# Idle matmuls of 512 columns cut into quarters at the head of TensorE's stream, to move its instruction fetches by 102 instructions

## The chip, the cores and the metric

One core of one Trainium2 chip. The metric is the device time of one execution in microseconds (us), as the median of several; the profile's span, from the first to the last instruction, is some 2 us shorter.

## The reference

```python
batch, m, k, h, n = 16, 512, 768, 3072, 768        # x, w1, b1, w2: float32
y = np.matmul(x, w1) + b1
y = 0.5 * y * (1.0 + erf(y / np.sqrt(2.0)))        # exact GELU
return np.matmul(y, w2).astype(np.float32)
```

## The kernel before

Both products run in f16 by a scheme with seven instead of eight block products (the second in two levels), so VectorE forms sums of operands all the time and ScalarE and VectorE combine partial results. All instructions stand in an order fixed by hand. While the first tiles of x are on their way, TensorE runs idle matmuls on zeros (`spin`), from 1.19 us on. Its clock rises meanwhile: up to 4.63 us the idle matmuls of 512 columns start 427 ns apart, and later ones 216 (the record of the granted clock begins at 4.63 us, at 1.0); the dense matmuls begin at 10.06 us.

```python
for t in range(4):                                   # x tiles 0 to 3, by the hardware DMA queue
    nc.sync.dma_start(out=xf[:, t, :], in_=xr[:, t, :])
...
load_wt(1)                                           # w1 tile 1, by the software queue (POOL)
for t in range(4, 8):
    load_x(0, t)                                     # x tiles 4 to 7, the same queue
for n in range(2, 4):
    load_wt(n)

def spin(n):
    for k in range(n):
        nc.tensor.matmul(out=(bX[1], bY[1])[k % 2][:], lhsT=zero[:, 0, 0:P], rhs=zero[:, 0, :],
                         start=True, stop=True, skip_group_check=True)

spin(9)
for t in range(4):
    ...                                              # cast of x tile t on VectorE
    transpose_pe(0, t, ...)                          # six transposes on TensorE, then a copy
    ...
    spin(2)
...
class Unit1:                                         # dense matmuls of the first product
    def mm(self, p, dst, first, c0, c1):
        ...
        for c in range(c0, c1):
            nc.tensor.matmul(out=dst[:, 0:RH], lhsT=w1_op(self.wt, slot)[:, c, :],
                             rhs=a[:, c, :], start=first and c == 0, ...)
...
    def store(self, r):                              # output stores of the second product
        ...
        eng = nc.sync if self.sb + 1 == nsb and self.p != 2 else nc.gpsimd
        eng.dma_start(out=orr[...], in_=self.dst[:, r]...)
```

Of the kernel before, what the change touches and what calls it, by code (L numbers as in the profile page):

```python
# [10 lines left out]
P = 128  # L11
# [11 lines left out]
def kernel(  # L23
# [8 lines left out]
    nc = tc.nc  # L32
# [5 lines left out]
    RH = SB // 2  # L38
# [160 lines left out]
    bX = [pp.tile([P, 512], FP32, name=f"bX{k}") for k in range(2)]  # L199
    bY = [pp.tile([P, 512], FP32, name=f"bY{k}") for k in range(2)]  # L200
# [4 lines left out]
    with tc.manual_schedule():  # L205
# [539 lines left out]
        for half in range(2):  # L745
            r = slice(half * KQ, (half + 1) * KQ)
            nc.sync.dma_start(out=wf[:, r, :], in_=w1r[:, r, 0:2 * P])
        nc.scalar.dma_start(out=bf, in_=b1.rearrange("(hc p) -> hc p", p=P))
        zero = XTs[1][:, 0]
# [11 lines left out]
        def spin(n):  # L761

            for k in range(n):
                nc.tensor.matmul(out=(bX[1], bY[1])[k % 2][:], lhsT=zero[:, 0, 0:P], rhs=zero[:, 0, :],
                                 start=True, stop=True, skip_group_check=True)

        spin(9)
        for t in range(4):
            xhs[t] = xh_of(0, t)
            nc.vector.tensor_copy(out=xhs[t], in_=xf[:, t, :])  # L770
            transpose_pe(0, t, copy_halves if t == 3 else nc.scalar.copy)
            if t == 0:
                nc.tensor.transpose(out=bW[:, 0:2 * NH], in_=bf, identity=idf[0:2 * NH, 0:2 * NH])
                nc.scalar.copy(out=b1t[:], in_=bW[:, 0:2 * NH])
            spin(2)
# [402 lines left out]
```

## Time and profile before

| | before |
|---|---|
| median | 852.18 us (852.14 to 852.53, 3 runs) |
| span of the profiled run | 850.5 us |
| TensorE busy | 99% of the span |
| dense matmuls begin | 10.06 us |
| last matmul starts | 845.02 us |
| from there to the end of the span ("tail") | 5.50 us |
| instruction fetches of TensorE | 51 packets of 16384 bytes; the first at 19.24, the second at 38.73, the last at 844.30 us |

TensorE sets the time between the head and the tail, and the last matmul's start plus the tail is the span (845.02 + 5.50): what delays the last matmul and what comes after it can be read apart. The prediction below shows most of the lines behind this table. One thing that it shows only in numbers is how SyncE issued the last four output stores (start us, us that the issue took, queue, line, what):

```profile
842.54 0.37 SPq L550 DMA_DIRECT2D out_dram<-arena  x1
843.91 0.37 SPq L556 DMA_DIRECT2D out_dram<-arena  x1
844.90 1.04 SPq L550 DMA_DIRECT2D out_dram<-arena  x1
846.04 0.42 SPq L529 DMA_DIRECT2D out_dram<-arena  x1
```

Three issues take about 0.4 us and one 1.04. It starts while the last instruction fetch runs (844.30 to 845.54).

### The profile page before, as it was taken

The numbers are of one execution on the slowest core, as the hardware profiler recorded it, in microseconds if no ns is written. First come the engines' busy times: TensorE is split into PE (matmuls) and PEld (weight loads), VectorE is DVE, ScalarE is ACT, GpSimd is POOL, SyncE is SP. The second block draws the span as 40 slices with busy tenths as digits, with TensorE's granted clock in tenths as the row PEclk, the third lists the DMA queues.
The fourth block names the chain that finished last, engine by engine and source line by source line (L and its number), as shares of the span: only waits on it lengthen the run. The fifth ranks groups of instructions, "written<-read, shape, count | busy, mean of one in ns | idle before, by whom it ended". The sixth has DMA issues, their size and how long they took to land.

```text
span 850.5 us, 16682 instructions
## 1 busy us (share of the span) xinstructions
PE 842.8 (99%) x6504; PEld 573.4 (67%) x6504; DVE 673.3 (79%) x1134; ACT 426.3 (50%) x700; POOL 94.8 (11%) x151
## 2 busy tenths in 40 slices
PE   8999999999999999999999999999999999999997
PEld 5444445796544897449964599545995469944797
DVE  5766679777857997679967799668996699957997
ACT  4777763231287413773247721577126861277511
POOL 5021100042200002000020000210002100010000
PEclk9999999999999999999999999999999999999999
DMA  9998796699998699977999599995999949984497
GB/s 224 203 282 173 163 222 230 235 203 219 368 340 185 216 338 364 290 163 266 335 366 292 125 298 342 360 288 108 316 350 347 259 143 323 359 308 146 122 316 255
DMA packets 144819, 222.11 MB, mean 261 GB/s; under 512 B 61964, under 2 KB 85444, under 8 KB 144740
## 3 DMA queue, kind: packets, MB, share of 16 engines
q1 hardware_dynamic: 117392, 178.85, 66.6%
q0 software_dynamic: 27168, 42.08, 22.3%
q8 instruction: 51, 0.84, 0.4%
q14 instruction: 28, 0.23, 0.1%
q10 hardware_dynamic: 180, 0.11, 0.0%
HBM read 181.78 MB, written 49.45 MB: 272 GB/s over the span
## 4 chain that ended last, share of the span: by engine, by line
PE 98%; DMA 1%; ACT 0%; DVE 0%; SPq 0%; issue 0%
PE bY L414 21%; PE bY L518 15%; PE bX L414 14%; PE bX L518 10%; PE bW L414 7%; PE bZ L414 7%; PE bZ L518 5%; PE bW L518 5%; PE bY L457 4%; PE bZ L457 2%; PE bW L457 2%; PE bY L606 2%; PE bX L606 1%; PE bX L457 1%; DMA arena<-in_x_dram 1%; PE bZ L606 1%
## 5 line engine op out<-in xcount | busy, mean ns | idle before, releaser
L210 DVE TENSOR_TENSOR arena<-arena 128x1536 f16<-128x1536 f16 (+6 forms) x638 | 410.1, 674 | 5.7 <-ACT arena L335 0.9
L414 PEld LDWEIGHTS <-arena 128*128 128x128 f16 x1974 | 192.5, 98 | 224.0 <-issue 0.2
L518 PEld LDWEIGHTS <-arena 128*128 128x128 f16 x3528 | 292.1, 98 | 8.2
L414 PE MATMUL bY<-arena 128*128 128x512 f16 x846 | 214.4, 379 | 0.0
L637 DVE TENSOR_TENSOR arena<-bY,arena 128x512 f32<-128x512 f32 (+1 forms) x102 | 69.4, 681 | 118.1 <-PE bY L414 88.0
L630 ACT COPY bY<-bX 128x512 f32<-128x512 f32 (+1 forms) x145 | 79.6, 549 | 118.1 <-DVE arena L567 87.9
L518 PE MATMUL bY<-arena 128*128 128x192 f16 x1500 | 138.3, 246 | 0.0
L414 PE MATMUL bX<-arena 128*128 128x512 f16 x564 | 138.2, 379 | 0.0
L430 ACT ACTIVATE arena<-arena,b1t 128x1024 f16<-128x1024 f32 x94 | 108.0, 1149 | 51.6 <-DVE arena L665 51.6
L650 ACT COPY arena<-bW 128x512 f32<-128x512 f32 (+1 forms) x149 | 81.9, 550 | 92.9 <-PE bW L518 43.9
L518 PE MATMUL bX<-arena 128*128 128x192 f16 x1020 | 93.1, 246 | 0.0
L665 DVE TENSOR_TENSOR arena<-bZ,arena 128x512 f32<-128x512 f32 (+1 forms) x102 | 69.3, 679 | 21.4 <-PE bZ L414 18.2
L550 POOL DMA_DIRECT2D out_dram<-arena x42 | 30.5, 728 | 409.7 <-DVE arena L661 374.1
L414 PE MATMUL bW<-arena 128*128 128x512 f16 x282 | 76.2, 379 | 0.0
L414 PE MATMUL bZ<-arena 128*128 128x512 f16 x282 | 76.2, 379 | 0.0
L681 ACT COPY bZ<-bY 128x512 f32<-128x512 f32 (+1 forms) x60 | 31.8, 529 | 80.8 <-PE bY L457 30.0
L435 ACT ACTIVATE arena<-bX,b1t 128x512 f16<-128x512 f32 x94 | 64.0, 680 | 9.8 <-PE bX L414 9.7
L435 ACT ACTIVATE arena<-bY,b1t 128x512 f16<-128x512 f32 x94 | 63.3, 674 | 0.0
L457 PEld LDWEIGHTS <-arena 128*128 128x128 f16 x432 | 42.2, 98 | 28.0 <-issue 0.2
L319 POOL DMA_DIRECT2D arena<-in_x_dram x60 | 33.5, 626 | 156.3 <-DMA arena<-arena 146.9
L518 PE MATMUL bZ<-arena 128*128 128x192 f16 x504 | 48.5, 246 | 0.0
L518 PE MATMUL bW<-arena 128*128 128x192 f16 x504 | 48.5, 246 | 0.0
(63 smaller groups left out, 426.4 us busy)
## 6 DMA issues: line engine op xcount, KB each, us to landing
arena<-w2s SPq DMA_DIRECT2D x299, 288.0 KB, 4.6
arena<-w1s SPq DMA_DIRECT2D x72, 672.0 KB, 6.8
out_dram<-arena POOLq DMA_DIRECT2D x46, 384.0 KB, 7.1
w2s<-arena SPq DMA_DIRECT2D x49, 288.0 KB, 4.4
arena<-in_x_dram POOLq DMA_DIRECT2D x60, 192.0 KB, 7.7
w1s<-arena SPq DMA_DIRECT2D x12, 672.0 KB, 6.6
arena<-in_w_dram POOLq DMA_DIRECT2D x17, 384.0 KB, 8.4
out_dram<-arena SPq DMA_DIRECT2D x13, 384.0 KB, 2.5
```

What stands on the lines that cost most here:

```text
L210: nc.vector.tensor_tensor(out=o, in0=a, in1=b, op=op)
L319: nc.gpsimd.dma_start(out=xhs[t], in_=xr[:, sb * 8 + t, :])
L414: nc.tensor.matmul(out=dst[:, 0:RH], lhsT=w1_op(self.wt, slot)[:, c, :], rhs=a[:, c, :], start=first and c == 0, stop=c == self.C - 1, ski ...
L430: nc.scalar.activation(out=self.G[1][:, hi, :, :], in_=self.tmp, func=GELU, bias=b1t[:, 2 * hi + 1:2 * hi + 2])
L435: nc.scalar.activation(out=self.G[0][:, hi, row, :], in_=bank[:, 0:RH], func=GELU, bias=b1t[:, 2 * hi:2 * hi + 1])
L457: nc.tensor.matmul(out=dst[:, 0:N2], lhsT=a, rhs=w[:, :, c, :], start=first and c == 0, stop=c == self.C - 1, skip_group_check=True)
L518: nc.tensor.matmul(out=dst[:, t * N4:(t + 1) * N4], lhsT=a, rhs=w[:, c, :], start=first and c == 0 and t == ts[0], stop=c == NQ - 1, skip_ ...
L606: nc.tensor.matmul(out=dst[:, t * N4:(t + 1) * N4], lhsT=a, rhs=self.w[q][:, c, :], start=first and c == 0 and t == 0, stop=c == NQ - 1, s ...
L630: nc.scalar.copy(out=bY[u.g % 2][:, 0:u.F], in_=bX[u.g % 2][:, 0:u.F])
L637: nc.vector.tensor_tensor(out=u.c22(), in0=bY[u.g % 2][:, 0:u.F], in1=w[:, 0:u.F], op=ADD)
L650: nc.scalar.copy(out=w[:, 0:u.F], in_=bW[:, 0:u.F])
L665: nc.vector.tensor_tensor(out=u.c12(), in0=bZ[:, 0:u.F], in1=w[:, 0:u.F], op=ADD)
```

## The change

The idle matmuls stream the same columns, but each in four instructions with a weight load of their own. The work before the first real matmul should take the same time, and every later instruction stands 102 places further down, so that the fetches, which come some 255 instructions apart in the trace of before (on average; 51 of them for some 13,020 TensorE instructions), should fall 102 instructions sooner in the work.

```diff
         def spin(n):
             for k in range(n):
-                nc.tensor.matmul(out=(bX[1], bY[1])[k % 2][:], lhsT=zero[:, 0, 0:P], rhs=zero[:, 0, :],
-                                 start=True, stop=True, skip_group_check=True)
+                for r in range(0, RH, P):
+                    nc.tensor.matmul(out=(bX[1], bY[1])[k % 2][:, r:r + P], lhsT=zero[:, 0, 0:P],
+                                     rhs=zero[:, 0, r:r + P], start=True, stop=True,
+                                     skip_group_check=True)
```

## The prediction

Its sum came to 851.7 us (852.18 - 0.6 + 0.1). The pace that the prediction uses can be read off the trace of before between 11 and 845 us: matmuls of 128, 192, 256, 384 and 512 columns start on average 55.8, 82.6, 109.2, 162.5 and 215.9 ns after one of the same shape, which is 2.4 columns per ns plus 2.5 ns to within 0.2 ns. Up to 4.63 us, 512 columns took 427 ns; before has no row of 128 columns so early.

> **What bounds the kernel now.** I read the page's busy shares first, then TensorE's waits, then the chain of waits at the two ends of the span, and last the transfers there.
>
> ```profile
> span 850.5 us, 16682 instructions
> PE 842.8 (99%) x6504; PEld 573.4 (67%) x6504; DVE 673.3 (79%) x1134; ACT 426.3 (50%) x700; POOL 94.8 (11%) x151
> q8 instruction: 51, 0.84, 0.4%
> PE bX L764 <- DVE arena L750: 1.2, 1, 1.2
> PE bT L333 <- DVE arena L770: 0.7, 1, 0.7
> PE bT L333 <- ACT arena L335: 0.4, 1, 0.4
> ```
>
> TensorE is busy for 99% of the span and its three listed waits all lie in the first 10 us (the third column of a wait is the longest one). I also took the start-to-start distances of all 6504 matmuls from the trace and set each against the pace at which its shape runs in a stream (columns at 2.4 per ns plus 2.5 ns, which 512 columns keep at 216 ns). After 10.06 us only nine distances exceed it by over 30 ns, 0.65 us together, and six of those are one recurring place, "bX to bY" of the second product. So between 10 and 845 us TensorE loses nothing to its instruction fetches: the 51 fetches (0.84 MB, so 16 KB each) do not stall it. What a change to the fetches can win must then lie outside this stretch. That leaves the head and the tail.
>
> The head, in the chain of waits (start us, us, what):
>
> ```profile
> 1.67 5.22 DMA arena<-in_x_dram
> 6.89 0.02 issue
> 6.92 0.65 DVE arena L770
> 7.57 0.05 issue
> 7.62 0.52 PE bT L333 x6
> 8.14 0.02 issue
> 8.16 0.81 ACT arena L335
> 8.97 0.01 issue
> 8.98 0.52 PE bT L333 x6
> 9.50 0.02 issue
> 9.53 0.49 ACT arena L329
> 10.01 0.04 issue
> 10.06 0.81 PE bX L786 x3
> ```
>
> The idle matmuls (L764) are not in it. The arrival of x, its cast on VectorE, the transposes and ScalarE's copy set 10.06 us, where the dense matmuls begin. The idle matmuls fill TensorE's time beside that.
>
> The tail, by stretches (the last two columns are the mean busy share of the 16 DMA engines, and GB/s), and the transfer queues from 844.2 to 845.6 us:
>
> ```profile
> 844.30:845.55 1.25, 0.97 (x12) 0.74 (x9) 1.11 (x4) 0.00 (x0) 0.00 (x0) 1.00 0.94 327
> 845.85:846.29 0.44, 0.00 (x0) 0.00 (x0) 0.00 (x0) 0.00 (x0) 0.00 (x0) 1.00 0.05 14
> 846.30:848.25 1.95, 0.00 (x0) 0.00 (x0) 0.00 (x0) 0.00 (x0) 0.00 (x0) 0.86 0.89 308
> 848.30:849.00 0.70, 0.00 (x0) 0.00 (x0) 0.00 (x0) 0.00 (x0) 0.00 (x0) 0.50 0.06 21
> q8 instruction: 1, 0.02, 5.5%
> ```
>
> The last matmul starts at 845.0 us; from there on the output stores set the end. The last instruction fetch lies in the middle of them: one packet of 16384 bytes from 844.30 to 845.54 us. While it runs, the engine that carries it does no stores: of the store that ends then, 15 of 16 completion writes come by 845.25 us and one is missing. From 845.85 to 846.29 us fifteen engines have nothing to do and one catches up (a share of 0.05 is 0.8 of 16 engines). In the last stretch a share of 0.06 is again one engine of 16: its packets follow one another to 848.97 us, while those of the others end at 848.26 to 848.28. The sum fits: 1.24 us lost, some 0.44 caught up in the lull, 0.7 left over. The last landings read 848.65 us (the last of the even ones), then 849.03, 849.24 and 849.44 from the late engine. The program's end waits for the 849.44.
>
> [...]51 packets of 16384 bytes for some 13,020 TensorE instructions, on average 256 apart (single distances are 190 to 324). [...]That a long fetch holds up the store packets of its one engine is my reading of the tail above[...].[...]
>
> **The change part by part.** 17 idle matmuls (9, then 2 after each of four transposed tiles) become 68 of a quarter of the size. Columns and banks stay as they were. Added: 51 matmuls and 51 weight loads, 102 TensorE instructions at the head; the other engines' order is the same line for line.
>
> *The opening nine.* Before: starts 427 ns apart from 1.19 us; the clock doubles at 4.63 us (the granted clock in the trace). After: 107 ns apart (427/4), 32 of the 36 by 4.63 us, the last 4 in 0.22 us, so the transposes of tile 0 start at about 4.85 us against 4.83. Zero. If a cold weight load (151 ns by its record) did not hide, 23 would be done by 4.63 and the other 13 at 98 ns would take until 5.9 us. Tile 0 would then be one microsecond late; tile 2 waits for its x until 7.56 us and would start at most 0.3 us late, and tile 3 (8.98) has 0.59 us of idle TensorE ahead of it. So it would mostly be absorbed.
>
> *The four pairs.* 8 quarters at 55.6 are 0.44 us against 0.43. Ahead of 7.62, 8.98 and 10.06 us TensorE is idle for 0.88, 0.59 and 0.30 us, so the last pair may take 0.73 us, or 91 ns for each quarter. [...]Zero.
>
> *The fetches.* Each falls 102 instructions earlier in the work. I count that against the index of the instruction that runs as a fetch comes. For the last one: 13001 in the old numbering becomes 12899, which runs at 840.2 us. One standard deviation of the distances from the 256 grid is 21 instructions, here 0.9 us, so 839.3 to 841.1 us. Stores resume at 840.56 us after two idle microseconds of the queue. A fetch of about 0.95 us (its length on a quiet queue) from 840.2 makes its engine 0.6 us late at 841.15; the gap at 841.75 to 841.88 gives back 0.13 and the lull at 845.85 to 846.29 another 0.44. So next to nothing is left at the end: minus 0.79 us (849.44 to 848.65). If the fetch starts at 841 or later, 0.95 to 1.2 us are lost, minus 0.57 returned, leaving 0.4 to 0.6, so a gain of only 0.2 to 0.4. I take 0.6 us as the mean.
>
> The first fetch moves from 19.24 us to between 11 and 13.8 us (old index 133 runs at 13.6), into the loads of x tiles 4 to 7, which fill the queue (127% of the engines between 10 and 14 us, two of them at a time). These complete at 12.63, 13.58, 14.54 and 15.49 us, and their transposes start at 13.29, 14.27, 15.26 and 17.06, some 0.7 us later. A late engine (0.95 us) would stall TensorE by 0.25 us once. I count half of that, plus 0.1.
>
> Between, 49 fetches move by 4 to 11 us. None stalls TensorE today wherever it falls, so I count 0.
>
> Sum: 852.18 - 0.6 + 0.1 = 851.7 us.
>
> **The rivals.** (1) *Nothing happens*: the fetches are 0.4% of the transfers and TensorE never waits for one, so the time stays 852.2 within 0.2. For it: the 99%. Against it: the one late engine at the end. (2) *The quarters cost more than they hide*: cold or warm pairs issue-bound[...]. [...]Against it: pairs of 192 columns run at 82.5 ns, so two instructions cost no more than 41 each to issue, and the head's chain does not hold the idle matmuls.[...] (3) *A moved fetch strikes a load that a matmul is about to need*, in the head (+0.25) or in the middle (a few tenths): 852.0 to 852.4. (4) *The full gain without the cost*: 851.4.
>
> **Range and chances.** The reachable gain is 0.8 us, under 0.1% of the time, and the three runs of before spread by 0.39 us. The gain of 0.2 to 0.8, the head's cost of 0 to 0.25 and 0.2 of run-to-run noise give 851.1 to 852.2; for a stall in the middle or a costlier head I open the top to 852.4 and the bottom to 851.0. A change of 2% is 17 us, which nothing here can make: 1% either way.
>
> **What would show it.** In the profile after: the last matmul starts at 845.0 within 0.3; the clock rises near 4.63; dense matmuls begin at 10.06; the last fetch starts between 839 and 841.5; the last stretch with one busy engine is gone or shorter than 0.3 us, and the last landings lie together near 848.7; the span is about 850.0. The prediction is wrong if the tail keeps its late engine (then it was not the fetch), if a fetch still falls after 844 us, or if the dense matmuls begin later than 10.3.

## The result, and the profile after

The changed kernel took 852.16 us (851.62 to 852.5, 6 runs) against 852.16 (851.82 to 852.53, 6 runs) of the kernel before in the same rounds: ratio 0.9999, 95% interval 0.9987 to 1.0012. (A ratio is the mean time of one kernel's fast runs over that of the other's of the same rounds, so not quite the ratio of the medians.) So the time stayed, inside the range of the prediction and 0.46 us above its point.

The profile did not stay. The first line of its page, TensorE's waits, and the last fetch (queues between 839.5 and 840.6 us), where L414 is line 414 of the kernel:

```profile
span 850.0 us, 16784 instructions
PE bX L765 <- DVE arena L750: 1.2, 1, 1.2
PE bT L333 <- DMA arena<-in_x_dram: 0.8, 1, 0.8
PE bY L414 <- DVE bZ L683: 0.3, 1, 0.3
q8 instruction: 1, 0.02, 5.0%
```

There are still 51 fetches, now at 12.58, 30.19 and so on, the last at 839.63. Two waits are new: transposes wait for x itself, and dense matmuls (L414) for VectorE.

The tail in stretches that stand to the last matmul (845.92, it was 845.02) about as those of before, and SyncE's last four issues (start us, us that the issue took, queue, line, what):

```profile
845.20:846.45 1.25, 0.97 (x12) 0.74 (x9) 1.11 (x4) 0.00 (x0) 0.00 (x0) 1.00 1.00 350
846.75:847.19 0.44, 0.00 (x0) 0.00 (x0) 0.00 (x0) 0.00 (x0) 0.00 (x0) 1.00 1.02 365
847.20:849.15 1.95, 0.00 (x0) 0.00 (x0) 0.00 (x0) 0.00 (x0) 0.00 (x0) 1.00 0.65 214
849.20:849.90 0.70, 0.00 (x0) 0.00 (x0) 0.00 (x0) 0.00 (x0) 0.00 (x0) 1.00 0.00 0
```

```profile
843.44 0.37 SPq L550 DMA_DIRECT2D out_dram<-arena  x1
844.82 0.37 SPq L556 DMA_DIRECT2D out_dram<-arena  x1
845.80 0.37 SPq L550 DMA_DIRECT2D out_dram<-arena  x1
846.27 0.44 SPq L529 DMA_DIRECT2D out_dram<-arena  x1
```

The late engine is gone (a share of 0.00 where it was 0.06), but so is the lull (1.02 where it was 0.05), because the third issue is back at 0.37 us and the fourth store follows 0.47 us after it instead of 1.14. The tail fell from 5.50 to 4.10 us: 0.67 us from the issue, and the other 0.73, by subtraction, from the late engine.

The head gave that back. The matmuls that wait, and what VectorE waited for (the number in brackets is the engine's idle time before the instruction), in the changed kernel:

```profile
14.73 0.29 PE L333 MATMUL bT<-ident,arena 128*128 128x128 f16 x2 [0.76 <-DMA arena<-in_x_dram]
37.34 0.36 DVE L210 TENSOR_TENSOR arena<-arena 128x384 f16<-128x384 f16 x1 [1.14 <-DMA arena<-in_w_dram]
39.93 0.38 PE L414 MATMUL bY<-arena 128*128 128x512 f16 x1 [0.32 <-DVE bZ L683]
```

and in the kernel before:

```profile
14.27 0.22 PE L333 MATMUL bT<-ident,arena 128*128 128x128 f16 x1
36.38 1.14 DVE L210 TENSOR_TENSOR arena<-arena 128x384 f16<-128x384 f16 x3 [0.66 <-DMA arena<-in_w_dram]
38.98 0.38 PE L414 MATMUL bY<-arena 128*128 128x512 f16 x1
```

The same transposes start 0.46 us later, the sum on VectorE that needs a w1 tile 0.96 us later, and the matmuls that wait for VectorE behind it 0.95 us later; the last matmul is 0.90 us later. By start-to-start distance the two stalls are 0.92 and 0.48 us; the dense matmuls had begun 0.49 us sooner (9.57 us), which the first stall ate.

The completions of x tile 5 show how: in the changed kernel 15 of its 16 writes come from 12.66 to 13.32 us and the last at 14.27, while the fetch runs from 12.58 to 13.54. Before, all came from 12.86 to 13.56. Each write shows in the trace as an event of the semaphore that the waiting engine counts on, about 0.35 to 0.4 us later; the tile's last event is at 14.68 in the changed kernel, 0.05 us ahead of its transposes, and was at 13.93, 0.34 us ahead of them.

So the theory after the result: *fetches 1 and 2 now strike loads that TensorE waits for, the last no longer strikes the stores, and the two cancel.* Rivals: the profiles differ by chance; or the small idle matmuls themselves slow the head.

### The profile page after: what moved, and what is told of

It reads as the page before. It is cut to its first block, busy times and chain, and to the rows that moved or that the text cites. A ratio compares the mean times of both kernels' runs of the same rounds, so it can differ in the third digit from the quotient of the medians.

```text
span 850.0 us, 16784 instructions
## 1 busy us (share of the span) xinstructions
PE 843.8 (99%) x6555; PEld 577.8 (68%) x6555; DVE 673.6 (79%) x1134; ACT 426.6 (50%) x700; POOL 94.8 (11%) x151
## 4 chain that ended last, share of the span: by engine, by line
PE 95%; DMA 4%; DVE 0%; POOL 0%; issue 0%; DVEq 0%
PE bY L414 21%; PE bY L518 15%; PE bX L414 14%; PE bX L518 10%; PE bZ L414 7%; PE bW L414 7%; PE bZ L518 5%; PE bW L518 5%; PE bY L457 4%; DMA arena<-in_x_dram 3%; PE bZ L457 2%; PE bW L457 2%; PE bY L606 2%; DMA arena<-in_w_dram 1%; PE bX L606 1%; PE bX L457 1%
## 5 line engine op out<-in xcount | busy, mean ns | idle before, releaser
L414 PEld LDWEIGHTS <-arena 128*128 128x128 f16 x1974 | 192.5, 98 | 224.5 <-issue 0.8
L414 PE MATMUL bY<-arena 128*128 128x512 f16 x846 | 214.4, 379 | 0.3 <-DVE bZ L683 0.3
L414 PE MATMUL bX<-arena 128*128 128x512 f16 x564 | 138.2, 379 | 0.0
L414 PE MATMUL bW<-arena 128*128 128x512 f16 x282 | 76.2, 379 | 0.0
L414 PE MATMUL bZ<-arena 128*128 128x512 f16 x282 | 76.2, 379 | 0.0
```

## The experiments

Twelve kernels ran, all with a correct result, five rounds each. They were built in four calls (e1 to e4, e5 to e8, e9 to e11, e12). The kernels of a call shared one chip and one set of runs of the kernel before; e5 to e8 were set against the nine such runs of the first call and one of their own (853.77 us), and e12 ran on another chip than e1 to e11. By the rule of 2% every one of them counts as "same"; the differences here are of a tenth of a per cent. One device serves most of them: cutting a 512-column dense matmul into two halves adds two instructions and costs, by the pace of before (109.2 ns for 256 columns, 215.9 for 512), 2.5 ns, so it shifts all later fetches without touching the head.

```diff
+        left = [51]
+
+        def pieces(g):
+            if g < 6 or left[0] == 0:            # from which unit on; how many
+                return [slice(0, RH)]
+            left[0] -= 1
+            return [slice(0, RH // 2), slice(RH // 2, RH)]
...
-                    nc.tensor.matmul(out=dst[:, 0:RH], lhsT=w1_op(self.wt, slot)[:, c, :],
-                                     rhs=a[:, c, :], start=first and c == 0, ...)
+                    for r in pieces(self.g):
+                        nc.tensor.matmul(out=dst[:, r], lhsT=w1_op(self.wt, slot)[:, c, :],
+                                         rhs=a[:, c, r], start=first and c == 0 and r.start == 0, ...)
```

All results first. A stall is a place after 11 us where two matmuls start over 0.15 us further apart than their pace; the last four columns are from the one profiled run of each.

| run | median us (runs) | before, set beside it | ratio (95%) | stalls: at, us | last matmul | tail us | last fetch |
|---|---|---|---|---|---|---|---|
| e1 before again | 852.74 (5) | 852.50 | 1.0001 (0.9989 to 1.0014) | none | 845.48 | 5.46 | 844.80 |
| e2 changed again | 852.19 (5) | 852.50 | 0.9997 (0.9984 to 1.0009) | 14.7: 0.94; 40.1: 0.69 | 846.12 | 4.09 | 840.06 |
| e3 51 halves from 38 us | 851.41 (5) | 852.50 | 0.9989 (0.9975 to 1.0002) | 57.1: 0.59 | 845.35 | 4.11 | 839.44 |
| e4 quarters and 77 halves | 853.89 (5) | 852.50 | 1.0016 (1.0004 to 1.0029) | 14.5: 1.60; 301.9: 0.16 | 846.49 | 5.41 | 846.14 |
| e5 51 halves from 98 us | 851.27 (6) | 852.51 | 0.9987 (0.9975 to 1.0) | none | 845.21 | 4.11 | 839.05 |
| e6 eighths | 851.81 (4) | 852.51 | 0.9995 (0.9982 to 1.0009) | none | 845.27 | 4.16 | 849.84 |
| e7 17 halves | 851.74 (4) | 852.51 | 0.9992 (0.9978 to 1.0006) | 38.6: 0.24 | 844.69 | 4.80 | 841.45 |
| e8 35 halves | 851.61 (5) | 852.51 | 0.9992 (0.9979 to 1.0006) | 38.9: 0.57 | 845.02 | 4.47 | 840.18 |
| e9 nine in quarters, 24 halves | 851.76 (5) | 852.50 | 0.9992 (0.9978 to 1.0006) | 41.8: 0.28 | 845.00 | 4.11 | 838.84 |
| e10 changed, third time | 851.98 (5) | 852.50 | 0.9993 (0.9979 to 1.0007) | 14.8: 0.51; 40.2: 0.73 | 846.26 | 4.10 | 839.98 |
| e11 as e5 | 851.11 (5) | 852.50 | 0.9985 (0.9972 to 0.9998) | 38.8: 0.18; 56.8: 0.16 | 845.12 | 4.09 | 838.87 |
| e12 as e9, 22 of the halves early | 852.11 (5) | 852.17 | 0.9994 (0.998 to 1.0007) | 12.9: 0.38; 39.8: 1.19 | 845.72 | 4.10 | 839.53 |

**e1 and e2: how much is chance.** No edit.

> The kernel before, unchanged, as a yardstick: ratio 1.000, with the spread of its executions. Theory (two fetches of the changed kernel strike loads in the head and cost 0.9 us, one no longer strikes the tail and gives 1.4 us): the profile repeats the first one of before, that is no stall over 0.2 us on TensorE between 11 and 845 us, last matmul within 0.2 us of 845.0, last fetch among the final stores, and 5.3 to 5.6 us from the last matmul's start to the end of the span. Rival (all of this is the spread of executions): last matmul and tail differ from the first profile by 0.5 us or more though nothing was changed.

> The changed kernel, unchanged. Theory: the profile repeats the first one of after: stalls of some 0.9 us near 14.7 us and 0.5 us near 39.9 us (less or more as x arrives late or early, but the matmuls after 40 us stand at the same times), last matmul at 845.9, tail 4.1 us. Rival: other stalls or none, last matmul near 845.0. If the granted clock again rises near 7 us and not near 4.6, the smaller idle matmuls do that; if it rises elsewhere, that is chance.

Both repeat their first profile in what matters: e1 has no stall and a tail of 5.46 us, with the issue of the last store but one again slow, at 1.12 us:

```profile
845.35 1.12 SPq L550 DMA_DIRECT2D out_dram<-arena  x1
```

e2 has both stalls and a tail of 4.09. What is chance: e1's last matmul came 0.46 us later than in the first profile, outside its expected 0.2, because its dense matmuls began at 10.45 instead of 10.06 us (x came later). And the clock: it rose at 4.63 and 5.37 us in the two profiles of before, at 7.05 and 5.77 in those of the changed kernel, and at 6.95 in e3, which has the old idle matmuls. So the quarters need not be what delays the clock. Nor do these profiles tie a late rise to small idle matmuls: the clock rose as late with the old kind, and earliest of all, at 4.12 us, in e6, whose idle matmuls are smaller still. In all 14 profiles, with the first matmul at 1.19 us, it rose between 4.12 and 7.05 us; what sets the time no run shows.

**e3 and e4: the two halves of the change apart.** e3: `spin` as before, 51 halves from unit 6. e4: the change, with 77 halves. (Both expectations say "from 45 us on"; in the profiles the halves run from 37.9 to 51.2 us in e3 and from 39.5 to 58.5 us in e4. In e3 fetch 2 came at 37.5, still ahead of them.)

> The idle matmuls as before; instead 51 dense matmuls from 45 us on are cut into halves of 256 columns, which adds the same 102 instructions after the first two fetches have come. Theory: fetches 1 and 2 as before (near 19 and 39 us) and no stall in the head; the later ones 102 instructions sooner and the last near 840 us, before the stores; last matmul at 845.0 plus 0.13 (51 times 2.5 ns), tail 4.1 us, span 849.3, time 850.9: ratio 0.9985. Rival that the tail gain is chance: tail 5.5, ratio 1.000.

> The quarters of the change, and 77 dense matmuls from 45 us on cut into halves: 256 instructions more in all, so fetches 1 and 2 come as in the changed kernel, the later ones where they came before (one fetch more in all). Theory: stalls of the head as in the changed kernel, last matmul near 846.0 (845.9 plus 0.2), last fetch among the final stores, tail 5.5: span 851.6, time 853.3, ratio 1.0013. Rival: no cost in the head, 852.3; or no late engine though a fetch lies in the stores, tail 4.1.

With e1 and e2 this is a table of two by two: the early fetches in the place of before or of the change, and the last one inside or ahead of the stores. (The upper left is the nine runs of the kernel before; e1's own five have 852.74.)

| medians | last fetch in the stores | last fetch ahead of them |
|---|---|---|
| fetches 1 and 2 late (as before) | 852.50 | 851.41 |
| fetches 1 and 2 early (as changed) | 853.89 | 852.19 |

Moving the last fetch gains 1.1 and 1.7 us; moving the first two costs 1.4 and 0.8. (The two gains, and the two costs, differ by 0.6 us, which is the size of the stall that e3 alone has, below.) The four come out in the expected order, within 0.6 us of the expected times. e4 shows the cost alone, and is the only kernel that is slower than the kernel before by its interval. Its profile has the stall and the fetch in the tail:

```profile
PE bT L333 <- DMA arena<-in_x_dram: 1.4, 1, 1.4
846.84 0.85 SPq L539 DMA_DIRECT2D out_dram<-arena  x1
```

Here the second fetch came at 31.08 us and the one early stall was 1.60 us long, so that TensorE was already late enough for the w1 tile. e3 had a stall that nobody expected, 0.59 us at 57.1 us, of which its profile puts 0.43 down to a load of w1; its third fetch had moved from 65 to 52.1 us.

**e5 and e11: a version meant to beat both.** As e3, with `g < 19` in place of `g < 6`, so that the halves begin near 98 us.

> As the third run (idle matmuls as before, 51 dense matmuls in halves), but the halves stand from some 98 us on, so fetches 1 to 4 all come as before. Theory: the third run's stall of 0.59 us at 57 us, which came after its third fetch had moved to 52 us, is gone; no stall over 0.2 us; last matmul 845.1 to 845.6 (the start of the dense matmuls varied by 0.4 us between two executions of the kernel before), tail 4.1, time 850.9 to 851.2, ratio 0.998 to 0.9985. Rival (the stall belongs to the halves, or to chance): it comes again at another place, 851.4.

> The kernel of the fifth run again, as it is the one that should beat both: tail 4.1, last matmul 844.8 to 845.6, stall at 39 us up to 0.6, ratio 0.9985 (0.9975 to 1.000) and 0.7 to 1 us under the changed kernel of the same rounds. If it was luck: 1.000.

The stall near 57 us is gone in e5 (0.16 us in e11, with the third fetch at 65.2, so part of it is not the fetch's). The tail is 4.1 in both. The issues of e5:

```profile
845.09 0.37 SPq L560 DMA_DIRECT2D out_dram<-arena  x1
845.55 0.44 SPq L539 DMA_DIRECT2D out_dram<-arena  x1
```

This kernel took 851.27 and 851.11 us, and in the second try, e11, its interval lies under 1. (The 0.9987 of e5 just misses the expected 0.998 to 0.9985.) Beside the changed kernel of the same rounds it is 0.87 us faster (851.11 against 851.98). That was e10, the changed kernel a third time, for which I had expected the stalls of e2, a last matmul at 845.9 to 846.2 and a ratio of 0.9996, or 1.000 if gain and cost cancel; it had both stalls, the first of only 0.51 us, its last matmul at 846.26, and 0.9993, whose interval does not tell the two apart. The kernel of e5 and e11 is the fastest, 0.13 to 0.15% under the kernel before; the first interval just reaches 1.0.

**e6: are the small matmuls at fault?** Pieces of 64 columns: 238 instructions more, near a whole period of 256.

```diff
-                for r in range(0, RH, P):
+                for r in range(0, RH, P // 2):          # and P // 2 in place of P in the slices of out and rhs
```

> The idle matmuls in eighths of 64 columns: 238 instructions more than before. As fetches come 256 apart, all but one extra fetch in the first microseconds fall 18 instructions later in the work than before. Theory (the fetch's place costs, not the small matmuls): no stall near 14.7 and 39.9 us, last matmul 845.0 to 845.6, last fetch near 845, among the last stores, so a tail of 5 us or more: 852.2 to 852.9, ratio 1.000 to 1.001. Rival (small idle matmuls themselves make the head slow): stalls again, last matmul at 846 or later, 853 or more.

The head came as the theory has it: matmuls even smaller than those of the change, fetches at 8.67 and 20.02 us, no stall, last matmul at 845.27. So it is the place of the fetch that costs. The tail missed my expectation: 18 instructions later did not bring the last fetch to 845 but to 849.84, when the stores had landed, and the tail was 4.16. The fetch may come after the stores as well as before. (One of the four runs took 853.4 us with a span of 850.0.)

**e7 and e8: where in the stores the fetch falls.** As e5 with `left = [17]` and `left = [35]`.

> As the fifth run with 17 matmuls in halves, 34 instructions: the last fetch comes near 843 us, in the middle of the stores that fill the queue from 841.9 to 845. Theory: its engine cannot catch up before the last stores are issued, so one issue of a store takes about 1 us instead of 0.37 and the tail stays at 5.2 to 5.5; time as before, ratio 1.000. Rival (any shift of the fetches off 844.3 is enough): tail 4.1, ratio 0.9985.

> As the fifth run with 35 matmuls in halves, 70 instructions: the last fetch comes near 841.5 us, as the stores begin. Theory: its engine is late by up to 1 us and the queue has only 0.13 us of gap before the last stores, so a tail between 4.4 and 5.4, near 4.1 only if the fetch happens to come before 840.6; ratio 0.9985 to 1.000. Rival: 4.1 at any place before 842.

e8's tail came as expected; e7's did not, since its last fetch came at 841.45 and not near 843 (in the profiles of before and after, the places of the fetches vary around a grid of 256 instructions by 21 and 20, one standard deviation). Ordered by the distance of the last fetch from the last matmul, all profiles but e6's make one row: 6.3 to 5.9 us ahead, tails of 4.09 to 4.11; 4.8 ahead, 4.47 (e8); 3.2 ahead, 4.80 (e7); 0.7 to 0.35 ahead, 5.41 to 5.50 (before, e1, e4). In e7 it is an earlier store whose issue is held up, with time left to recover:

```profile
842.21 1.12 SPq L560 DMA_DIRECT2D out_dram<-arena  x1
844.57 0.37 SPq L560 DMA_DIRECT2D out_dram<-arena  x1
```

Both also stalled near 38.8 us by 0.24 and 0.57, with fetch 1 where it was before and fetch 2 at 37.1 and 37.2 (38.1 and 38.7 in the kernel before). Their dense matmuls had begun early (9.36 and 9.29 us). In the kernel before, the matmul in question starts at 38.98 without a stall. So, by these profiles, the w1 tile lets it start at about 38.6 to 39.0 at the soonest, and the kernel before had next to no slack there.

**e9 and e12: the first and the second fetch apart.** e9 has quarters in the opening nine alone, and 24 halves from 98 us; e12 has 22 of these 24 between 21 and 26 us.

```diff
-        spin(9)
+        spin(9, P)                        # spin(n, w=RH): pieces of w columns; the pairs stay spin(2)
...
-        left = [24]                       # e9: from unit 19 on
+        left = {2: 22, 19: 2}             # e12: 22 from unit 2 on, 2 from unit 19 on
```

> Only the opening nine idle matmuls in quarters (54 instructions sooner), the pairs as before, and 24 matmuls from 98 us on in halves (48 more, 102 in all). Fetch 1 should come near 15.7 us, when x tiles 4 to 7 have landed, fetch 2 near 34 us, while the weight tile that the matmuls at 39 us need is on its way; the last near 839.5. Theory (each of the first two fetches costs by itself what it strikes): no stall near 14.7 us, a stall of 0.4 to 1.2 us near 39 to 40 us, matmuls after it at the place of the changed kernel, last matmul 845.8 to 846.3, tail 4.1, 851.8 to 852.2. Rival (the first fetch alone set both stalls, by way of later loads): no stall, last matmul 845.1, 851.2.

> As the ninth run, but 22 of the 24 halved matmuls stand between 22 and 27 us instead of after 98 us. Fetch 1 stays where the ninth run had it (16.5 us, no stall at 14.7), fetch 2 should move from 35.4 to some 30.5 us, as in the changed kernel; from then on all is as in the ninth run. Theory (fetch 2 by itself makes an engine late for the weight tile): the tile's last completion, 35.6 us in the ninth run and 36.9 to 37.2 in the changed kernel, comes at 36.4 or later, TensorE stalls near 39 to 40 us by 0.3 to 1.0, last matmul 845.6 to 846.2, tail 4.1. Rival (the second stall too was set by fetch 1 at 12.6): completion 35.6 to 35.9, no stall over 0.3 there, last matmul 845.0.

In e9 fetch 1 came at 16.54 us and TensorE waited nowhere near 14.7. (Its one stall, 0.28 us at 41.8, has no wait in the profile that explains it.) Fetch 2 came at 35.36 and not near 34, and did not make the w1 tile late: its last completion was at 35.58. So e9 shows what fetch 1 does and leaves fetch 2 open; the expected stall and the last matmul at 846 did not come. e12 moves fetch 2 alone, to 30.16 us. VectorE's wait for the tile and TensorE's behind it, in e9 (first line) and e12 (the other two), each from its timeline:

```profile
36.04 1.15 DVE L210 TENSOR_TENSOR arena<-arena 128x384 f16<-128x384 f16 x3 [0.75 <-DMA arena<-in_w_dram]
```

```profile
37.19 1.15 DVE L210 TENSOR_TENSOR arena<-arena 128x384 f16<-128x384 f16 x3 [1.84 <-DMA arena<-in_w_dram]
39.79 0.38 PE L425 MATMUL bY<-arena 128*128 128x512 f16 x1 [1.03 <-DVE bZ L694]
```

The tile's last completion moved from 35.58 to 36.72 us, the stall was 1.19 us (a little over what I had allowed; the 0.38 us at 12.9 came ahead of any fetch) and the last matmul came 0.72 us later than in e9. The rival, that fetch 1 had set both, falls by these two profiles; the timed runs do not resolve this step (ratios of 0.9992 and 0.9994).

Not only one engine is late with this tile when a fetch comes at 30.2 to 31.1 us. The middle one of its 16 completions lies at 35.2 to 35.6 us in the five profiles where it does (the first of after, e2, e4, e10, e12), and at 34.2 to 34.8 in the nine others. POOL was not held up: it had issued the tile by 25.5 us in the profiles of both before and after. SyncE was. Its third transpose by DMA (L325), in progress when the fetch comes, took in before (first line) and after:

```profile
26.23 5.75 SPq L325 DMA_TRANSPOSE arena<-arena  x1
26.22 6.77 SPq L325 DMA_TRANSPOSE arena<-arena  x1
```

In all five it took 6.71 to 6.95 us, in the nine others 5.68 to 6.00. While it runs, the traffic all but stops on all engines: from 31.5 to 31.9 us 20 packets moved in after, where before had 174. So it is an issue of SyncE that is held up, as in the tail. Why the packets of POOL's queue stop with it no run shows.

## Why the prediction was right, point by point

The time, 852.16 us, is in the range of 851.0 to 852.4, and "within 2%" was never in doubt. The point, 851.7, was 0.46 us low in the first comparison and nearer in the later ones, where the changed kernel was 0.3 and 0.5 us under the kernel before. By the profiles the account is: last matmul 846.10 (mean of three) against 845.25 (mean of two), +0.85; tail 4.10 against 5.48, -1.38; together -0.53 us. The timed runs of all three comparisons (-0.1, -0.3 and -0.6 us by their ratios) agree with that to within their spread of a microsecond.

Of the signs that it named, the last fetch at 839 to 841.5, the end of the stretch with one busy engine and the span of 850.0 came. The last matmul at 845.0 within 0.3 did not (845.92), nor did the clock's rise near 4.63 (7.05). And "dense matmuls later than 10.3", a sign of being wrong, would have struck the unchanged kernel (e1, 10.45). The sum for the upper end (gain 0.2, cost 0.25, noise 0.2) gives 852.4 and not 852.2; the range was opened to 852.4 for another reason.

1. *The idle matmuls cost nothing.* Right. A quarter took 107 ns before the clock rose and 56 ns after it; the dense matmuls began at 9.41 to 10.06 us against 10.06 and 10.45. e6 shows it with eighths.
2. *The last fetch moves to 840.2 us.* Right: 839.63, 840.06 and 839.98, against a last matmul that had moved too.
3. *Gain in the tail, 0.6 us and at most 0.79.* Right in kind, too small by more than half: 1.38. The term that failed is the sum "1.24 us lost, some 0.44 caught up in the lull, 0.7 left over". I took the lull for a thing that was there anyway and that gave time back. It was made by the fetch: while an engine was late, SyncE's issue took 1.04 instead of 0.37 us, and fifteen engines had nothing to do until the last store came. The four lines of SyncE's issues had it before.
4. *The first fetch moves into the loads of x tiles 4 to 7.* Right: 12.56 to 12.64 us. *It stalls TensorE by 0.25 us, of which half counts.* Too small: 0.51 to 0.94 us, in three profiles of three. The slack of "some 0.7 us" was measured from the completion write to the transposes, which start only after the semaphore event, some 0.4 us later. Of the 0.34 us between event and transposes in the kernel before, 0.05 were still needed in the changed one, so about 0.3 us were slack, and an engine 0.95 us late makes 0.65. The rest goes with the start of the dense matmuls: the earlier they begin, the longer TensorE then waits (0.92 and 0.94 after 9.57 and 9.41 us, 0.51 after 10.06).
5. *"Between, 49 fetches move by 4 to 11 us. None stalls TensorE today wherever it falls, so I count 0."* Wrong for one, by 0.48 to 0.73 us. That nothing waits today says nothing of how near it is to waiting: VectorE's own wait for that w1 tile, 0.66 us before the change, stood in its timeline, with TensorE right behind it. For the other 48 it held.
6. *Rival 1, "nothing happens"*, had the time right for a wrong reason: two effects of over 0.8 us each cancelled. *Rival 3* (a moved fetch strikes a load, 852.0 to 852.4) was the true course together with the gain, and I had given it 0.1 us in the sum.

So the range held because the two terms that I had sized too small, gain and cost, were too small by about the same: that is luck.

## What to carry to other kernels

In these kernels, instructions added to TensorE's stream moved the later fetches (102 at the head moved the last from 844.30 to 839.63 us). A fetch, one packet of 16384 bytes and 0.88 to 1.79 us in the profiles of before and after, made one of 16 engines about a microsecond late (0.95 us for x tile 5), and at times held up an issue of SyncE (1.04 and 1.12 us instead of 0.37 for a store). Here TensorE showed no stall over 0.15 us from that in e5, with 51 fetches; it lost time where a fetch met a transfer that was waited for with less slack (stalls of up to 1.60 us, in e4), or the last stores, on which the end of the program waits (1.38 us of the tail). So before moving fetches, look for such places along the whole stream, at the issuing sequencer and on the engine ahead of TensorE as well as at TensorE, and place the shift behind those that must not move: the same 102 instructions added after 98 us instead of in the head turned a draw into a gain of 0.13 to 0.15% (two tries, the interval clear of 1 in one).
